# One encoder layer: seven block products for the gate tiles behind attention, token mixes made during attention, the second FFN matrix mixed beside its own products

## The chip, the cores and the metric

The kernel runs on one core of a Trainium2 chip. The metric is the device time of one execution in microseconds (us). Engines carry the profile's names: PE is TensorE (matmuls; PEld its weight loads), DVE VectorE, ACT ScalarE, POOL GpSimd, SP SyncE, on whose queue nearly all transfers are issued.

## The reference

One layer on 1024 tokens of 1024 channels: a modulated norm, one projection to queries, keys, values and gates, two attentions (a neighbourhood of a 2-D grid, and sliding windows of three dilations), a merge of both by sigmoid gates, an output projection, and a SwiGLU feed-forward network (FFN) of width 2816.

```
h = rms_norm(x, g_norm1) * (1 + sc1) + sh1
qa, ka, va, qb, kb, vb, gates = split(h @ w_in)
...
gate_a, gate_b = split(sigmoid(gates + b_gate), 2)
merged = gate_a * (o_a @ w_proj_a) + gate_b * (o_b @ w_proj_b)
x = x + gt1 * (merged @ w_o)
h2 = rms_norm(x, g_norm2) * (1 + sc2) + sh2
a, up = split(h2 @ w_ffn_in, 2)
x = x + gt2 * ((silu(a) * up) @ w_ffn_out)
```

## The kernel before

**Precision.** Everything is float32. For a matmul each operand is split into a high and a low half of a rounded float32 (`wsplit`: the high half is a copy on ACT, L108; the low half is a subtraction on POOL or DVE, L109), and each product is three passes, hi x hi, hi x lo, lo x hi (`PASS`). A matmul takes 128 x 128 weights and 512 moving columns.

**Buffers.** A weight comes by SP into a ring of 6 buffers `raw` (`wload`, L101), and its halves stand in rings of 10 each, which is five steps of two operands. PSUM has four names (ps_s, ps_t, ps_v, ps_d) of two banks. Pools lie on the left or on the right side of the core's memory.

**Order.** TensorE's queue is kept in the order of the program. On DVE, ACT, POOL and SP a scheduler orders the instructions at build time, among those that are ready by its own simulation; each queue then runs in that order, so an instruction that waits holds up all behind it. What is marked with `keep_in_program_order` (pinned, below) stays in the program's order on its engine.

**Stages.** (1) x is normalised and transposed into hT (8 row groups of 128 channels, 1024 tokens, a high and a low tile). (2) Steps n = 0 to 91, eight to a unit (units 2 to 4 are n = 16 to 39), interleave the projections (L293), attention (L442 scores, L468 transposes of P, L472 the copies PT, L483 the products with the values) and small work, such as the norms of q and k (L311 to L316) and the columns of the modulation (L282). The last steps also compute half gates (L602) for the first channel tiles, kept in DRAM. (3) Behind attention, `gates` computes the other gate tiles: for tile i and branch br, one product of 8 row groups for each half of the tokens: 24 matmuls each (L580, `mm_set`), a sigmoid from PSUM. Beside it run `w2_combos`, which load the four blocks of the second FFN matrix a group, make four mixes and store them to DRAM, for 11 groups; `w1_combos`, the same for two groups of the first matrix; and at its end `o_split`, which splits the attention's output into oT. (4) The merge (L580 on oT), (5) the output projection, (6) the first FFN matrix, (7) the second.

**Seven products.** Both FFN matrices are multiplied by Winograd's form of Strassen's method: of a product of 2 x 2 blocks, seven block products of mixed operands instead of eight, with sums of the results. In the second matrix (`prod2`) one of the seven has 11 steps k, each of two operands (mixed activations from `ga_d`, and a block or a mix of the matrix), with four tiles m of 3 matmuls. The seven run one after the other, and DVE sums them from PSUM into four quadrants c11 to c22. `finish` multiplies a quadrant by gt2 on DVE (L1266), adds x on POOL (L1267) and stores it. In the last product the three last steps run tile by tile, and each tile ends with a multiplication, a sum and a store (L1298, L1299).

Of the kernel before, what the change touches and what calls it, by code (L numbers as in the profile page):

```python
# [27 lines left out]
LATE = (3, 4, 5, 6, 7)  # L28
# [4 lines left out]
NLAND = 22  # L33
W2C = {0: (0,), 1: (1,), 2: (2, 3), 3: (4,), 4: (5,), 5: (6, 7), 6: (8,), 7: (9,), 8: (10,)}
# [9 lines left out]
def hybrid_layer(ctx: ExitStack, tc: tile.TileContext, x, colp, wada1, wada2, bada2, wqkv, wg, wpa, wpb,  # L44
# [539 lines left out]
    NPRE = 11  # L584

# [27 lines left out]
    gw, gsig = {}, {}  # L613
    units = []
# [144 lines left out]
    for n in range(6, 92):  # L759
# [67 lines left out]
    for br in range(2):  # L827
        gate_w(3, br)
    ap_.release()

    sgp = pool("sig", "right")
    sig = {}

    def sig_tile(i, br):
        z = sgp.tile(wide, F32, tag="sg", bufs=10, name="sg")
        for hf in range(2):
            sig.setdefault((i, br, hf), z[:, hf * 512:hf * 512 + 512])
# [4 lines left out]
    sig[2, 1, 1] = sgp.tile([128, 512], F32, name="s2")  # L842
    lnd = pool("land", "right")

    def gates(i, br):
        gate_w(i, br)
        for hf in range(2):
            hs = slice(hf * 512, hf * 512 + 512)
            if i * 4 + br * 2 + hf < NPRE:
                continue  # L850
            pb = bank("ds"[br])
            for j in range(2):
                mm_set(pb, gw[i, br][j], hT, 4 * j, 4, 8, 4 * j, hs)
            nc.scalar.activation(sig[i, br, hf], pb, AF.Sigmoid, bias=bg_c[:, 8 * br + i:8 * br + i + 1])

    def sig_load(i, br, hf):
        if i * 4 + br * 2 + hf < NPRE:
            hs = slice(hf * 512, hf * 512 + 512)
            nc.sync.dma_start(sig[i, br, hf], sig_d[i, br][:, hs])
            nc.scalar.activation(sig[i, br, hf], sig[i, br, hf], AF.Sigmoid)  # L860
# [7 lines left out]
    def merge(i):  # L868
        merge_w(i)
        wa, wb = mw[i]  # L870
        for hf in range(2):
            hs = slice(hf * 512, hf * 512 + 512)
            ppa, ppb = bank("tv"[hf]), bank("ds"[hf])
            mm_set(ppa, wa, oT, 0, 4, 4, 0, hs)
            mm_set(ppb, wb, oT, 4, 2, 2, 0, hs)
# [7 lines left out]
    def o_split():  # L883
        for pr in (4, 5, 0, 1, 2, 3):
            for hf in range(2):
# [3 lines left out]
                hi, lo = oT[0][:, pr, hs], oT[1][:, pr, hs]  # L889
                if pr < 4:  # L890
                    hi, lo = (z[:, pr].rearrange("p (r w) -> p w r", r=16)[:, 32 * hf:32 * hf + 32] for z in oT)
                    raw = raw.rearrange("p (w r) -> p w r", r=16)
                nc.scalar.activation(hi, raw, AF.Copy)
                (nc.gpsimd if hf else nc.vector).tensor_sub(lo, raw, fview(hi))

    def w2_combos(k):
        b = {}
        for r in range(2):
            for c in range(2):
                b[r, c] = lnd.tile([128, 512], F32, tag="l", bufs=NLAND, name="l")  # L900
# [504 lines left out]
```

## Time and profile before

| what | value |
|---|---|
| median of 3 runs | 1545.73 us (1543.94 to 1547.7) |
| profiled execution: time, span | 1547.32 us, 1545.5 us |
| granted clock | 0.999 |
| busy: PE, DVE, ACT, POOL | 1523.5, 1009.0, 652.5, 635.5 us |
| gates behind attention | 628.22 to 742.72 us, 504 matmuls |
| second FFN matrix | from 1331.2 us to the end |

The span is the profile's, from the first instruction to the last; the execution's time has about 2 us more. A row of a group names line, engine, operation, output and inputs, count, then busy time and the mean of one in ns. In a timeline a row with x3 is three instructions run together.

### The profile page before, as it was taken

The numbers are of one execution on the slowest core, as the hardware profiler recorded it, in microseconds if no ns is written. First come the engines' busy times: TensorE is split into PE (matmuls) and PEld (weight loads), VectorE is DVE, ScalarE is ACT, GpSimd is POOL, SyncE is SP. The second block draws the span as 40 slices with busy tenths as digits, with TensorE's granted clock in tenths as the row PEclk, the third lists the DMA queues.
The fourth block names the chain that finished last, engine by engine and source line by source line (L and its number), as shares of the span: only waits on it lengthen the run. The fifth ranks groups of instructions, "written<-read, shape, count | busy, mean of one in ns | idle before, by whom it ended". The sixth has DMA issues, their size and how long they took to land.

```text
span 1545.5 us, 24656 instructions
## 1 busy us (share of the span) xinstructions
PE 1523.5 (99%) x8216; PEld 1280.4 (83%) x8216; DVE 1009.0 (65%) x2230; ACT 652.5 (42%) x1702; POOL 635.5 (41%) x618
## 2 busy tenths in 40 slices
PE   9999999999999999999999999999999999999998
PEld 7988888898888877888888888888888888888887
DVE  6776676776889843333475488678867776434477
ACT  5564555555545453224342254223322233344433
POOL 0422331221000031565352220577777777545555
PEclk9999999999999999999999999999999999999999
DMA  9323231443344252896445234344543334576765
GB/s 364 125 85 98 62 117 44 129 132 112 89 132 144 90 174 71 276 382 234 133 136 200 82 109 141 122 153 156 171 135 104 107 105 133 197 217 197 246 216 199
DMA packets 153950, 236.42 MB, mean 153 GB/s; under 512 B 27856, under 2 KB 65616, under 8 KB 153824
## 3 DMA queue, kind: packets, MB, share of 16 engines
q1 hardware_dynamic: 153824, 234.85, 47.1%
q8 instruction: 65, 1.06, 0.3%
q14 instruction: 61, 0.50, 0.1%
HBM read 175.95 MB, written 58.83 MB: 152 GB/s over the span
## 4 chain that ended last, share of the span: by engine, by line
PE 88%; DVE 4%; DMA 3%; issue 2%; ACT 2%; POOL 0%; SPq 0%; DVEq 0%; POOLq 0%; ACTq 0%
PE ps_d L293 14%; PE ps_v L1091 7%; PE ps_d L1091 7%; PE ps_s L1091 7%; PE ps_t L1091 6%; PE ps_s L580 5%; PE ps_d L580 4%; PE ps_d L602 4%; PE ps_d L1247 4%; PE ps_s L1247 4%; PE ps_v L1247 3%; PE ps_t L1247 3%; PE ps_v L483 2%; PE ps_s L442 2%; PE ps_d L1027 2%; PE ps_s L1027 2%
## 5 line engine op out<-in xcount | busy, mean ns | idle before, releaser
L109 POOL TENSOR_TENSOR wlo<-raw,whi 128x512 fp32r<-128x512 f32 (+2 forms) x214 | 281.6, 1323 | 483.5 <-ACT whi L108 403.0
L108 ACT ACTIVATE whi<-raw 128x512 fp32r<-128x512 f32 (+1 forms) x382 | 222.0, 601 | 272.6 <-PE ps_s L1247 42.4
L293 PE MATMUL ps_d<-whi,hT 128*128 128x384 f32 x1152 | 317.8, 344 | 1.3 <-ACT v L328 1.3
L109 DVE TENSOR_TENSOR wlo<-raw,whi 128x512 fp32r<-128x512 f32 (+1 forms) x168 | 155.7, 938 | 100.2 <-ACT whi L108 88.3
L293 PEld LDWEIGHTS ps_d<-whi,hT 128*128 128x128 f32 x1152 | 211.1, 189 | 7.0 <-ACT vs L331 3.5
L293 PE MATMUL ps_d<-wlo,hT 128*128 128x384 f32 x576 | 194.0, 337 | 0.0
L293 PEld LDWEIGHTS ps_d<-wlo,hT 128*128 128x128 f32 x576 | 108.9, 189 | 0.2 <-POOL wlo L109 0.2
L1041 POOL TENSOR_TENSOR e<-e,c 128x512 f32<-128x512 f32 x44 | 67.8, 1541 | 47.9 <-DVE c L1171 25.0
L108 ACT ACTIVATE whi<-ws 128x512 fp32r<-128x512 f32 x60 | 37.8, 630 | 116.3 <-DVE ws L1108 55.0
L323 POOL TENSOR_TENSOR ra<-qn,rtab 128x64 f32<-128x64 f32 x48 | 16.4, 342 | 167.2 <-DVE qn L316 125.5
L457 ACT ACTIVATE P<-P,st 128x256 f32<-128x256 f32 (+2 forms) x100 | 46.2, 463 | 69.5 <-DVE st L456 69.4
L314 DVE TENSOR_REDUCE ss<-sq 128x4 f32<-128x256 f32 x80 | 33.3, 416 | 47.4 <-ACT sq L311 47.3
L1091 PE MATMUL ps_v<-h2T,whi 128*128 128x512 f32 x192 | 59.3, 390 | 0.0
L1091 PE MATMUL ps_s<-h2T,whi 128*128 128x512 f32 x192 | 59.2, 390 | 0.0
L483 PE MATMUL ps_v<-PT,v 128*64 128x128 f32 (+1 forms) x672 | 55.0, 284 | 2.1 <-DVE PT L472 2.1
L1091 PE MATMUL ps_d<-h2T,whi 128*128 128x512 f32 x184 | 56.9, 390 | 0.0
L1039 ACT ACTIVATE e<-e 128x512 f32<-128x512 f32 x44 | 27.4, 630 | 69.2 <-DVE e L1174 47.3
L457 ACT ACTIVATE P<-P,sx 128x384 f32<-128x384 f32 (+1 forms) x64 | 37.1, 580 | 46.3 <-DVE sx L456 46.3
L468 PE MATMUL ps_t<-ident,P 128*128 128x128 f32 (+1 forms) x336 | 51.7, 275 | 4.0 <-DVE P L460 1.7
L442 PE MATMUL ps_s<-qk 64*128 64x256 f32 (+3 forms) x492 | 53.8, 321 | 1.8 <-DVE st L456 1.2
L602 PE MATMUL ps_d<-hT,whi 128*128 128x512 f32 x176 | 55.4, 396 | 0.0
L442 PEld LDWEIGHTS ps_s<-qk 64*128 64x128 f32 (+1 forms) x492 | 35.0, 182 | 23.7 <-issue 11.5
(369 smaller groups left out, 3913.9 us busy)
## 6 DMA issues: line engine op xcount, KB each, us to landing
raw<-in_w_dram SPq DMA_DIRECT2D x139, 256.0 KB
ga_d<-e SPq DMA_DIRECT2D x77, 256.0 KB
raw<-ga_d SPq DMA_DIRECT2D x77, 256.0 KB
wa<-in_wada_dram SPq DMA_DIRECT2D x32, 512.0 KB
raw<-in_wqkv_dram SPq DMA_DIRECT2D x80, 192.0 KB
l<-in_w_dram SPq DMA_DIRECT2D x52, 256.0 KB
w_d<-l SPq DMA_DIRECT2D x52, 256.0 KB
raw<-w_d SPq DMA_DIRECT2D x52, 256.0 KB
```

The lines of the kernel that those rows point to most:

```text
L108: nc.scalar.activation(hi[:, :n], r, AF.Copy)
L109: (eng or nc.gpsimd).tensor_sub(lo[:, :n], r, fview(hi[:, :n]))
L293: nc.tensor.matmul(pd[:, :384], tok(a, k, t), U.w[k][b][:, :384], start=(k == 0 and i == 0), stop=(k == KT - 1 and i == 2))
L442: nc.tensor.matmul(I.pS[h][:nq, :nk], U.qk[a][hs, I.q0:I.q0 + nq], U.qk[2 + b][hs, I.kb0 * 128:I.kb0 * 128 + nk], start=(i == 0), stop=(i ...
L457: nc.scalar.activation(P[:nq, :nk], P[:nq, :nk], AF.Exp, scale=-1.0, bias=nm, accum_out=sm)
L483: nc.tensor.matmul(po[hs, :nq], U.v[:, I.kb0 + i, hs], I.PT[h][:, i, :nq], start=(i == 0), stop=(i == nkb - 1))
L580: nc.tensor.matmul(pb, wsl[a][:, j * 128:(j + 1) * 128], src[b][:, ksrc + j, hs], start=(done == 0 and j == 0 and i == 0), stop=(done + j ...
L602: nc.tensor.matmul(st["p"], gw[i, br][j][a][:, kk * 128:(kk + 1) * 128], hT[b][:, k, hs], start=(k == 0 and q == 0), stop=(k == 7 and q == 2))
L1027: nc.tensor.matmul(pbs[hf], h2T[a][:, k, t * 128:(t + 1) * 128], wow[hf, k][b], start=(n == 0 and (a, b) == PASS[0]), stop=(n == KT - 1 an ...
L1041: nc.gpsimd.tensor_mul(sg, sg, up)
L1091: nc.tensor.matmul(pb, w[p][:, k * 128:(k + 1) * 128], b[q][:, k], start=(k == 0 and i == 0), stop=(k == 3 and i == 2))
L1247: nc.tensor.matmul(pb[m], o[0][a][:, m * 128:(m + 1) * 128], o[1][b], start=(k == 0 and i == 0), stop=(k == HT - 1 and i == 2))
```

## The change

**Gates.** Tiles 3 to 7 are computed by seven products a tile. The 2 x 2 blocks of the weights are two branches by two halves of the row groups; those of hT are two halves of the row groups by two halves of the tokens. A product has 4 row groups and 12 matmuls (`gate_mm`). The weight mixes are made on DVE for each tile (`gate_mixes`). The four mixes of hT are made once, in `t_piece`, which is called for 24 steps from n = 18 on: eight groups of three pinned pieces (two sums; three subtractions and a copy to the high half; two subtractions for the low half and two stores of 512 KB to `t_d`). Behind attention three pairs of tiles (`ttp`, right side) and one quarter of hT itself are loaded from `t_d`. DVE sums the products from PSUM, ACT adds the bias and takes the sigmoid of 1024 columns. Tiles 6 and 7 run interleaved, and the buffers of `ttp`, once free, hold oT. All low halves of `o_split` are on DVE. NPRE goes from 11 to 12: half gate (2, 1) of the second half of the tokens is computed in step n = 91.

**First FFN matrix.** The two `w1_combos` go from the gates' stage to n = 85 and 88, all on DVE.

**Second FFN matrix.** `w2_combos`, their stores and the later loads from `w2_d` go. `w2_mix` loads four blocks of a group during the second and third product, mixes them with four subtractions on DVE, and keeps the mixes in memory. The three products on unmixed blocks come first, with both operands' low halves on DVE; the last quadrant is now c21.

The diff, cut to its core ("..." where lines are left out):

```diff
@@ constants @@
-NLAND = 22
-W2C = {0: (0,), 1: (1,), 2: (2, 3), 3: (4,), 4: (5,), 5: (6, 7), 6: (8,), 7: (9,), 8: (10,)}
+TP0 = 18
+LATE, NPRE = (3, 4, 5, 6, 7), 12
@@ new helpers before the units @@
+    def gate_raw(i, q):
+        return wload(wg[i, :, 4 * q:4 * q + 4, :], 512)
+
+    def gate_mm(pb, w, b, k):
+        for q, (x, y) in enumerate(PASS):
+            nc.tensor.matmul(pb, w[x][:, k * 128:(k + 1) * 128], b[y][:, k],
+                             start=(k == 0 and q == 0), stop=(k == 3 and q == 2))
+    def t_piece(m):
+
+        (kk, pc), part = divmod(m // 3, 2), m % 3
+        if part == 0:
+            tpc["t"] = [big("tp", [128, 4, 256], F32R) for _ in range(2)]
+        hi, lo = tpc["t"]
+        y = fview(lo)
+        pin = tc.keep_in_program_order
+        if part == 0:
+            for c in range(2):
+                cs = slice(512 * c + 256 * pc, 512 * c + 256 * pc + 256)
+                pin(nc.vector.tensor_add(y[:, 2 * c:2 * c + 2], *(fview(h[:, kk:8:4, cs]) for h in hT)))
+        elif part == 1:
+            pin(nc.vector.tensor_sub(y[:, 0:3:2], y[:, 2:4], y[:, 0:3:2]))
+            pin(nc.vector.tensor_sub(y[:, 3], y[:, 3], y[:, 0]))
+            pin(nc.vector.tensor_sub(y[:, 1], y[:, 1], y[:, 3]))
+            pin(nc.scalar.activation(hi, y, AF.Copy))
+        else:
+            for a in (0, 2):
+                pin(nc.vector.tensor_sub(lo[:, a:a + 2], y[:, a:a + 2], fview(hi[:, a:a + 2])))
+            for q, z in enumerate((hi, lo)):
+                nc.sync.dma_start(t_d[q, :, :, kk, 256 * pc:256 * pc + 256].rearrange("s p c -> p s c"), fview(z))
@@ the steps of the units @@
+        if TP0 <= n < TP0 + 24:
+            t_piece(n - TP0)
+        if n in (85, 88):
+            w1_combos((n - 85) // 3, EARLY[(n - 85) // 3])
@@ behind attention @@
+    def gate_first(i, eng):
+        for q, nm in enumerate(("w11", "w12")):
+            gwt[i, nm] = wsplit(gate_raw(i, q), eng)
+
+    def gate_mixes(i, order):
+        r = {q: gate_raw(i, q) for q in (0, 2, 3, 1)}
+        s1 = wp.tile([128, 512], F32, tag="raw", bufs=NRAW, name="ws")
+        nc.vector.tensor_sub(r[0], r[0], r[2])
+        nc.vector.tensor_add(s1, r[2], r[3])
+        nc.vector.tensor_sub(r[2], r[3], r[0])
+        nc.vector.tensor_sub(r[1], r[1], r[2])
+        z = {"x1": s1, "x2": r[2], "x3": r[0], "w22": r[3], "x4": r[1]}
+        for nm in order:
+            gwt[i, nm] = wsplit(z[nm], nc.vector)
+    GORD, GLATE = ("x2", "x3", "x1", "w22", "x4"), ("w22", "x3", "x2", "x1", "x4")
+    for i in (3, 4):
+        gate_first(i, None)
+    tbg = {"w11": hblk(0, 0), "w12": hblk(1, 0), "x4": hblk(1, 1), "x1": hblk(0, 1)}
+    for nm in ("w22", "x3", "x2"):
+        tbg[nm] = [ttp.tile([128, 4, 512], F32R, tag="t", bufs=6, name="tg") for _ in range(2)]
+    for n, nm in ((3, "x2"), (2, "x3"), (0, "x1"), (1, "w22")):
+        for q in range(2):
+            nc.sync.dma_start(fview(tbg[nm][q]), t_d[q, n])
+    def gate_prod(i, nm, late=False):
+        ng[0] += 1
+        p = bank("tvds"[ng[0] % 4])
+        for k in range(4):
+            gate_mm(p, gwt[i, nm], tbg[nm], k)
+        c11, c12, c21, c22 = sig[i, 0, 0], sig[i, 0, 1], sig[i, 1, 0], sig[i, 1, 1]
+        add = nc.vector.tensor_add
+        if nm == "w11":
+            nc.scalar.activation(c12, p, AF.Copy)
+        elif nm == "w12":
+            add(c11, c12, p)
+        elif nm == "x4":
+            add(c12, c12, p)
+        elif nm == "w22":
+            if late:
+                nc.scalar.activation(c21, p, AF.Copy)
+            else:
+                add(c21, c21, p)
+        elif nm == "x3":
+            if late:
+                add(c21, c21, p)
+                nc.scalar.activation(c22, p, AF.Copy)
+            else:
+                add(c21, c12, p)
+        elif nm == "x2":
+            add(c12, c12, p)
+            if late:
+                add(c21, c21, c12)
+                add(c22, c22, c12)
+        else:
+            add(c22, c22 if late else c21, p)
+            add(c12, c12, p)
+
...
-    def w2_combos(k):
-        b = {}
-        for r in range(2):
-            for c in range(2):
-                b[r, c] = lnd.tile([128, 512], F32, tag="l", bufs=NLAND, name="l")
-                nc.sync.dma_start(b[r, c], w2[(k + HT * r) * 128:(k + HT * r + 1) * 128, c * 512:c * 512 + 512])
-        t1, t3, t2, t4 = b[0, 0], b[0, 1], b[1, 1], b[1, 0]
-        nc.gpsimd.tensor_sub(t1, b[0, 1], b[0, 0])
-        nc.vector.tensor_sub(t3, b[1, 1], b[0, 1])
-        nc.gpsimd.tensor_sub(t2, b[1, 1], t1)
-        nc.vector.tensor_sub(t4, b[1, 0], t2)
-        for n, z in enumerate((t1, t2, t3, t4)):
-            nc.sync.dma_start(w2_d[n, k], z)
...
-    GS = [(2, 1)] + [(i, br) for i in LATE for br in range(2)]
-    for n, z in enumerate(GS):
-        for y in GS[n:n + 3]:
-            gate_w(*y)
-        gates(*z)
-        for k in W2C.get(n, ()):
-            w2_combos(k)
-        if n in (3, 6):
-            w1_combos(n // 6, EARLY[n // 6])
-        if n == max(W2C):
-            lnd.release()
-            op_ = pool("o", "right")
-            oT = [op_.tile([128, 6, S], F32R, name=f"oT{i}") for i in range(2)]
-            o_split()
+    gate_first(5, nc.vector)
+    for i in (3, 4):
+        firsts(i)
+    gate_mixes(3, GORD)
+    firsts(5)
+    for i in (3, 4):
+        gate_first(i + 3, nc.vector)
+        for nm in GORD:
+            gate_prod(i, nm)
+        gate_end(i)
+        gate_mixes(i + 1, GORD)
+        firsts(i + 3)
+    for nm in GORD:
+        gate_prod(5, nm)
+    gate_end(5)
+    gate_mixes(6, GLATE)
+    gate_mixes(7, GLATE)
+    for nm in GLATE:
+        for i in (6, 7):
+            gate_prod(i, nm, True)
+    oT = {}
+    o_split()
+    for i in (6, 7):
+        gate_end(i)
@@ second FFN matrix @@
+    def w2_mix(k):
+        b = [w2p.tile([128, 512], F32, name=f"m{n}_{k}") for n in range(4)]
+        for z, (r, c) in zip(b, ((0, 0), (0, 1), (1, 1), (1, 0))):
+            nc.sync.dma_start(z, w2blk(r, c, k))
+        t1, t3, t2, t4 = b
+        nc.vector.tensor_sub(t1, t3, t1)
+        nc.vector.tensor_sub(t3, t2, t3)
+        nc.vector.tensor_sub(t2, t2, t1)
+        nc.vector.tensor_sub(t4, t4, t2)
+        w2m[k] = t1, t2, t3, t4
-    PRODS = ((0, lambda k: w2blk(0, 0, k)), (4, lambda k: w2_d[1, k]), (1, lambda k: w2blk(1, 0, k)),
-             (5, lambda k: w2_d[2, k]), (3, lambda k: w2_d[0, k]), (2, lambda k: w2_d[3, k]),
-             (6, lambda k: w2blk(1, 1, k)))
+    PRODS = ((0, (0, 0)), (1, (1, 0)), (6, (1, 1)), (4, 1), (3, 0), (5, 2), (2, 3))
+        g, m = PRODS[n]
+        a = wload(ga_d[g, k], 512)
+        b = w2m[k][m] if n > 2 else wload(w2blk(*m, k), 512)
+        return wsplit(a, nc.vector), wsplit(b, nc.vector if n < 3 or k == HT - 1 or (n == 6 and k > 4) else None)
+            if n in (1, 2) and k % 2 == n - 1:
+                w2_mix((k + (n - 1) * HT) // 2)
...
+    p7 = prod2(5)
+    for m in range(4):
+        add(c21[m], c21[m], p7[m])
+        add(c22[m], c22[m], p7[m])
     finish(1, 1, c22)
-    p4 = prod2(5)
-    for m in range(4):
-        nc.vector.tensor_add(c21[m], c21[m], p4[m])
-    finish(1, 0, c21)
-    finish(0, 1, c12, True)
-    p3 = prod2(6)
+    finish(1, 0, c21, True)
+    p4 = prod2(6)
     for m in range(4):
         tm = fp.tile([128, 512], F32, tag="tm", bufs=4, name="tmf")
-        nc.vector.tensor_mul(tm, p3[m], gt2[:, 512:])
-        nc.vector.tensor_add(tm, tm, c12[m])
-        nc.sync.dma_start(out[m * 128:(m + 1) * 128, 512:], tm)
+        nc.vector.tensor_mul(tm, p4[m], gt2[:, :512])
+        nc.vector.tensor_add(tm, tm, c21[m])
+        nc.sync.dma_start(out[(m + 4) * 128:(m + 5) * 128, :512], tm)
```

Where the instructions move, on three queues; `L` numbers are those of the kernel named.

VectorE in attention, step n = 18. Before (`ss4` and `rz` belong to the norms of q and k, `acc2` to the modulation's columns, `PT` is the copy of the transposed P):

```order
L314 TENSOR_REDUCE ss4_1940<-sq_1937 128x4
L263 TENSOR_TENSOR row_1927<-ps_t_1925,brow_1928 1x512
L280 TENSOR_SCALAR acc2_1934<-wa2_1932,cact_95 128x512
L120 TENSOR_SCALAR rv_1942<-ss4_1940 128x4
L282 SCALAR_TENSOR_TENSOR acc2_1934<-wa2_1932,cact_95,acc2_1934 128x512
L122 TENSOR_TENSOR rz_1944<-ry_1943,rv_1942 128x4
```

And of the change (`tp` is a piece of mixed tokens):

```order
L313 TENSOR_REDUCE ss4_1940<-sq_1937 128x4
L262 TENSOR_TENSOR row_1927<-ps_t_1925,brow_1928 1x512
L279 TENSOR_SCALAR acc2_1934<-wa2_1932,cact_95 128x512
L119 TENSOR_SCALAR rv_1942<-ss4_1940 128x4
L281 SCALAR_TENSOR_TENSOR acc2_1934<-wa2_1932,cact_95,acc2_1934 128x512
L637 TENSOR_TENSOR tp_2037<-hT0_105,hT1_390 128x512
L121 TENSOR_TENSOR rz_1944<-ry_1943,rv_1942 128x4
L637 TENSOR_TENSOR tp_2037<-hT0_105,hT1_390 128x512
L122 SCALAR_TENSOR_TENSOR rz_1944<-rz_1944,ry_1943 128x4
```

The piece's two sums stand among the small operations of a norm.

VectorE in the second product of the second FFN matrix, of the change, the row that follows ScalarE's first copy of product 1 (`wlo_15418`) and on (`m0_2` is the first mix of group 2):

```order
L108 TENSOR_TENSOR wlo_15418<-raw_15411,whi_15417 128x512
L1331 TENSOR_TENSOR m1_2_15446<-m2_2_15447,m1_2_15446 128x512
L1332 TENSOR_TENSOR m2_2_15447<-m2_2_15447,m0_2_15445 128x512
L108 TENSOR_TENSOR wlo_15438<-raw_15433,whi_15437 128x512
L1333 TENSOR_TENSOR m3_2_15448<-m3_2_15448,m2_2_15447 128x512
L108 TENSOR_TENSOR wlo_15442<-raw_15435,whi_15441 128x512
...
L1333 TENSOR_TENSOR m3_10_15956<-m3_10_15956,m2_10_15955 128x512
L108 TENSOR_TENSOR wlo_15618<-raw_15613,whi_15617 128x512
L108 TENSOR_TENSOR wlo_15622<-raw_15615,whi_15621 128x512
```

The last two rows are the low halves of that product's eleventh step; the mixes of all eleven groups stand ahead of them. Before, no mix stood on this queue in this stage.

SyncE where the second matrix begins, of the change (`ga_d` from `e` is a store of the first matrix's last results):

```order
L1146 DMA ga_d_75<-e_14840 128x512
L1146 DMA ga_d_75<-e_14821 128x512
L100 DMA raw_15313<-ga_d_75 128x512
L1146 DMA ga_d_75<-e_14975 128x512
L100 DMA raw_15315<-in_w2_dram 128x512
L100 DMA raw_15349<-ga_d_75 128x512
L100 DMA raw_15351<-in_w2_dram 128x512
L1328 DMA m0_0_15325<-in_w2_dram 128x512
L1328 DMA m1_0_15326<-in_w2_dram 128x512
```

The first load of a mix stands behind the last of these stores and behind the raw buffers of the second product's second step.

More of the change, by code (lines that the diff above doesn't have):

```diff
@@ L825, in hybrid_layer @@
             proj_post(U, t)
-    for br in range(2):
-        gate_w(3, br)
+    def gate_first(i, eng):
[14 more added lines that the diff above has]
+        gate_first(i, None)
     ap_.release()
     sgp = pool("sig", "right")
+    ttp = pool("tt", "right")
     sig = {}
+    tbg = {"w11": hblk(0, 0), "w12": hblk(1, 0), "x4": hblk(1, 1), "x1": hblk(0, 1)}
[4 more added lines that the diff above has]
+            nc.sync.dma_start(fview(tbg[nm][q]), t_d[q, n])
     def sig_tile(i, br):
@@ L841, in hybrid_layer, with sig_load, gate_end @@
             sig_tile(i, br)
[L842 to L860, printed above, removed]
+    def sig_load(i, br):
+        z = sig_tile(i, br)
+        nc.sync.dma_start(z, sig_d[i, br])
+        nc.scalar.activation(z, z, AF.Sigmoid)
+    ng = [0]
+    def gate_prod(i, nm, late=False):
[30 more added lines that the diff above has]
+            add(c12, c12, p)
+    def gate_end(i):
+        for br in range(2):
+            z = sig[i, br]
+            nc.scalar.activation(z, z, AF.Sigmoid, bias=bg_c[:, 8 * br + i:8 * br + i + 1])
     mw = {}
@@ L873, in merge @@
             ppa, ppb = bank("tv"[hf]), bank("ds"[hf])
-            mm_set(ppa, wa, oT, 0, 4, 4, 0, hs)
-            mm_set(ppb, wb, oT, 4, 2, 2, 0, hs)
+            for pb, w, prs in ((ppa, wa, (0, 1, 2, 3)), (ppb, wb, (4, 5))):
+                for j, pr in enumerate(prs):
+                    for q, (a, b) in enumerate(PASS):
+                        nc.tensor.matmul(pb, w[a][:, j * 128:(j + 1) * 128], oT[pr][:, b, hs],
+                                         start=(j == 0 and q == 0), stop=(j == len(prs) - 1 and q == 2))
             m, sb = sig[i, 0, hf], sig[i, 1, hf]
@@ L884, in o_split @@
         for pr in (4, 5, 0, 1, 2, 3):
+            oT[pr] = ttp.tile([128, 2, S], F32R, tag="t", bufs=6, name="oT")
             for hf in range(2):
@@ L963, in hybrid_layer @@
         for z in MSIG.get(n, ()):
-            sig_tile(*z)
-            for hf in range(2):
-                sig_load(*z, hf)
+            sig_load(*z)
         if n + 2 < 8:
@@ L972, in hybrid_layer @@
             wo_keep(MKEEP[n])
-    op_.release()
+    ttp.release()
     wop = pool("wo", "right")
@@ L1209, in hybrid_layer @@
         late_weights(j)
-    for j in EARLY + tuple(i for k in range(len(EARLY) // 2, HT) for i in (k, k + HT)):
+    for n, j in enumerate(EARLY + tuple(i for k in range(len(EARLY) // 2, HT) for i in (k, k + HT))):
         if j not in EARLY[:2]:
@@ L1227, in w2blk @@
         return w2[(k + HT * r) * 128:(k + HT * r + 1) * 128, c * 512:c * 512 + 512]
[L1229 to L1231 removed]
+    w2p = pool("w2m", "right")
+    w2m = {}
+    def w2_mix(k):
[9 more added lines that the diff above has]
+    PRODS = ((0, (0, 0)), (1, (1, 0)), (6, (1, 1)), (4, 1), (3, 0), (5, 2), (2, 3))
     LASTK = 3
     def operands(n, k):
[L1235 to L1236 removed]
+        g, m = PRODS[n]
+        a = wload(ga_d[g, k], 512)
+        b = w2m[k][m] if n > 2 else wload(w2blk(*m, k), 512)
+        return wsplit(a, nc.vector), wsplit(b, nc.vector if n < 3 or k == HT - 1 or (n == 6 and k > 4) else None)
     def blocks(name):
```

70 lines of the change are left out of this document (40 added, 30 removed).

## The prediction

> **What bounds the kernel now.** I read the page first (span, busy row, shares of the chain of waits), then the chain in order of time around the gates, then windows of the stages that the change touches, and last the timelines of VectorE, ScalarE and SyncE at the second FFN matrix.
>
> ```profile
> span 1545.5 us, 24656 instructions
> PE 1523.5 (99%) x8216; PEld 1280.4 (83%) x8216; DVE 1009.0 (65%) x2230; ACT 652.5 (42%) x1702; POOL 635.5 (41%) x618
> PE 88%; DVE 4%; DMA 3%; issue 2%; ACT 2%; POOL 0%; SPq 0%; DVEq 0%; POOLq 0%; ACTq 0%
> ```
>
> TensorE is busy for 99% of the span. Everything else is either hidden by matmuls or one of the few stalls among them. So a change gains where matmuls go, and loses where an operand of a matmul comes later than its matmul.
>
> The chain in order of time (start, length, engine, tile, line, count), end of attention to the merge; the two rows at 97x and 98x are from the first FFN matrix:
>
> ```profile
> 618.04 5.46 PE ps_d L602 x24
> ...
> 628.22 5.71 PE ps_s L580 x24
> 633.92 10.88 PE ps_d L580 x48
> ...
> 731.84 10.88 PE ps_s L580 x48
> 742.72 2.81 PE ps_t L580 x12
> ...
> 974.27 2.81 PE ps_v L1091 x12
> ...
> 982.61 2.73 PE ps_t L1091 x12
> ```
>
> The gates behind attention are one unbroken run of matmuls from 628.22 to 742.72: 114.5 us for 24 + 10 x 48 = 504 of them. Two prices show. On hT a matmul costs 10.88/48 = 0.2267 us; on oT, a tile of the right side of the memory, 2.81/12 = 0.2342. The rows of the first FFN matrix have the same pair: 2.81 where the moving operand is a mixed tile, 2.73 where it is h2T.
>
> The windows (stretch, length, then busy us and count of PE, PEld, DVE, ACT, POOL, then granted clock, DMA share, GB/s):
>
> ```profile
> 20.00:24.00 4.00, 4.00 (x44) 3.11 (x48) 2.46 (x7) 3.41 (x8) 0.00 (x0) 1.00 1.04 398
> 133.00:290.00 157.00, 152.87 (x1079) 135.76 (x1076) 105.56 (x375) 84.23 (x318) 42.63 (x111) 1.00 0.33 100
> 450.00:500.00 50.00, 49.97 (x363) 43.63 (x362) 47.29 (x159) 26.24 (x88) 3.19 (x3) 1.00 0.47 140
> 628.00:685.00 57.00, 57.00 (x255) 47.04 (x252) 21.95 (x19) 14.41 (x22) 37.80 (x28) 1.00 0.99 358
> 690.00:700.00 10.00, 10.00 (x46) 8.29 (x45) 3.75 (x4) 1.38 (x2) 7.08 (x6) 1.00 1.05 393
> 1331.00:1361.00 30.00, 30.00 (x134) 24.86 (x133) 12.87 (x14) 14.86 (x25) 19.82 (x15) 1.00 0.82 273
> 1361.00:1391.00 30.00, 30.00 (x134) 24.86 (x133) 9.51 (x15) 13.34 (x24) 13.20 (x10) 1.00 0.70 202
> ```
>
> In the gates (628 to 685) TensorE never stops and VectorE is idle for more than half, but the DMA engines are full (0.99). In both products of the second FFN matrix (1331 to 1391) nothing is near its limit: one product takes 30 us, VectorE works 10 to 13 of them.
>
> **The change, part by part. Gates.** Seven products of 4 x 3 = 12 matmuls on four row groups, 84 a tile, take the place of two halves a branch, 96; five tiles make 420 for 480. The 24 matmuls of half gate (2,1) move into the tail of attention, where the row at 618.04 prices them at 5.46. Of the 420, products w11, w12, x4 and x1 read hT itself (240 x 0.2267 = 54.4); x2, x3 and w22 read tiles of the right side, like oT (180 x 0.2342 = 42.2). Sum: 5.5 + 54.4 + 42.2 = 102.0 against 114.5, **-12.5 us**. Had all 420 the higher price it would be 114.5 - 5.5 - 98.4 = -10.7, with the lower -13.8.
>
> What must hide under these matmuls: the weight mixes, lo halves and sums of a tile, about 18 VectorE operations of 0.6, 11 us of the 84 x 0.23 = 19.3 that a tile lasts; the 6 MB of mixed tokens, at the 393 GB/s of 690:700, 16 us, the first pair of them, x2's, after a third of that plus some 4 for the release of attention's memory, about +10, where x2 is wanted after six products of 2.72, at +16.3; the split of o, whose three pairs of buffers come free 22, 16 and 11 us before the gates' end. In exchange the 44 loads and 44 stores of the second matrix's mixes (22 MB) leave, which filled the DMA engines here. I cost the covers at 0; had x2's pair landed last of the three, at 4 + 16 = +20, the price would be 4.
>
> **Pieces in attention.** Eight groups of three pinned pieces in steps n = 18 to 41, one a step. A group has five VectorE operations of 512 elements a partition and two of 256, one ScalarE copy of 1024 and two stores. The prices:
>
> ```profile
> L316 DVE TENSOR_TENSOR qn<-qn,ry 128x256 f32<-128x256 f32 x80 | 34.4, 429 | 2.8
> 1479.39 0.68 DVE L1287 TENSOR_TENSOR c<-c,ps_d 128x512 f32<-128x512 f32 x1
> 1479.98 0.68 DVE L1288 TENSOR_TENSOR c<-c,ps_d 128x512 f32<-128x512 f32 x1
> ```
>
> The last two start 0.59 apart, so a row of 512 costs about 0.6 and one of 256 between 0.33 (half of 0.68) and 0.43. A group is 5 x 0.6 + 2 x 0.33 = 3.7, all eight 29.6 us. The window 133:290 holds these steps: VectorE goes from 105.6 to 135 of 157, from 67 to 86%. A VectorE queue is kept in order, so behind a piece wait the norms of q and k, the maxima of the scores and the copies PT, which the next step's matmuls need. The bounds are 0 and 29.6/2 = 14.8, half of it exposed. I take +1, since the window 450:500 shows the same kind of steps with VectorE 95% busy and TensorE still at 49.97 of 50. The clause moving the first matrix's mixes into n = 85 and 88 puts eight operations there; I cost it at 0 behind 618.04's matmuls, at 4 if bare.
>
> **Second matrix.** The 44 subtractions of 11 groups now stand in product 2, and the first three products split both operands on VectorE. By the new order all of them come before the last lo half of product 2: 44 + 21 VectorE rows in that product, 44 + 18 loads on SyncE. A product's step is 30/11 = 2.73, so that lo is due 21 x 2.73 = 57.3 us after the first product began at 1331.2. The rows of the start:
>
> ```profile
> 1331.20 0.39 PE L1247 MATMUL ps_d<-whi 128*128 128x512 f32 x1
> 1347.23 2.12 SPq L1053 DMA_DIRECT2D ga_d<-e  x2
> 1349.43 0.38 SPq L101 DMA_DIRECT2D raw<-w_d  x1
> 1359.44 1.12 ACT L1274 ACTIVATE c<-ps_d 128x512 f32<-128x512 f32 x2
> ```
>
> VectorE: ScalarE evacuates the first product at +28.2 (1359.44), and in the new order the hi half of product 2's fourth step stands behind the first of those copies. The lo of that half is row 2212 of VectorE, at about +29.2; 50 rows follow to the one that is due, 50 x 0.597 = 29.9: +59.1, 1.8 late. DMA: the first mix load stands on SyncE behind the first matrix's last stores, which end at 1347.23 + 2.12 = +18 here, and behind the raw buffers of product 2's second step; I take +15.5, between +13.6 (a ring's step earlier) and +20. Then 62 x 262 KB at 393 GB/s, 0.667 each, is 41.4, landing 3.1 (the span's end less the last operation at 1541.72 + 0.69) and the two halves of the split 1.2: +61.2, 3.9 late. Both limits lie close to the due time, one above the other, not summed. I take **+3**; ends 1.4 (start at +13.6 with 398 GB/s: 13.6 + 40.8 + 4.3 = +58.7) and 11.5, worked out with the rivals.
>
> The Trainium skill, DMA: Bandwidth & Descriptors, Where 436 GB/s comes from, says that for transfers between HBM and SBUF the HBM side binds, at about 358 GB/s a core. By that the 62 loads take 45.4 us, 4 more, and the whole would end near 1543. The rows 398 and 393 above, loads and loads with stores of this kernel alone on its core, disagree with it, so the sum keeps 393; a lower rate as a mechanism is the first rival, priced from a row of this case.
>
> The last product:
>
> ```profile
> 1487.68 4.08 DVE L1266 TENSOR_TENSOR c<-c,gt 128x512 f32<-128x512 f32 x3
> 1520.03 10.38 DVE L109 TENSOR_TENSOR wlo<-raw,whi 128x512 fp32r<-128x512 f32 x8
> 1531.19 2.73 DVE L109 TENSOR_TENSOR wlo<-raw,whi 128x512 fp32r<-128x512 f32 x4 [0.78 <-ACT whi L108]
> 1536.81 4.09 PE ps_s L1247 x18
> 1541.72 0.69 DVE L1299 TENSOR_TENSOR tmf<-tmf,c 128x512 f32<-128x512 f32 x1
> PEld ps_v L1247 <- DVE wlo L109: 0.2, 1, 0.2
> ```
>
> At 1520 eight lo halves run back to back, so VectorE is behind there, and TensorE's whole wait for it is 0.2. The change finishes two quadrants here (c22 and c21) in place of one: four more sums of 0.6 and four more multiplications, 0.6 alone and 4.08/3 = 1.36 beside GpSimd: 4.8 to 7.8 us more in the same queue. Against it, the lo halves that GpSimd contended for (1.3 instead of 0.7) gain about 3.3. Net 1.5 to 4.5, of which the wait shows what is beyond the slack; I take **+1.5**, ends 0 and 4.7. After it the same multiply, add and store end the span.
>
> Sum: -12.5 + 1 + 3 + 1.5 = **-7.0**, on the profiled execution's 1547.3 (1545.5 span and 1.8 around it): 1540.3. That execution lies 1.6 above the median of 1545.73, so the forecast beside the median is 1545.7 - 7.0 = **1539 us**.
>
> **Rivals.** *The second product starves on loads.* At the rate of 1331:1361, 273 GB/s at share 0.82, a full queue is 273/0.82 = 333: 62 x 0.787 = 48.8, with 15.5 + 4.3 gives +68.6, 11.5 late. For it: these loads share the engines with stores there. Against: 393 with stores in the gates. Net -12.5 + 1 + 11.5 + 1.5 = +1.5, or, starting at +20 with 393 and the last product at 4.7, -12.5 + 1 + 8.4 + 4.7 = +1.6: no change, 1546 to 1547. Chance 0.22.
>
> *The pieces stall attention.* In-order VectorE puts its extra 29.6 us before work that matmuls wait for. Half exposed is 14.8 in place of 1: -7.0 + 13.8 = +6.8, 1552. It turns the sign from a loss of 8 on, some 27% of the pieces. For it: in 133:290 TensorE already misses 4.1 of 157. Against: 450:500. Chance 0.14.
>
> *Everything is hidden.* The loads start before +12 and VectorE's rows don't stand behind the evacuation; the pieces and the last product's rows fit their slack: -12.5 alone, 1533. Chance 0.06. *The products don't get cheaper than the matmuls they drop*: with every matmul at the right side's price, -10.7, it is 1541, inside the forecast.
>
> **How the numbers follow.** Forecast (-10 to -3.1) 0.58, everything hidden 0.06, no change 0.22, attention stalls 0.14. About 0.2%, 3.1 us, is what a measurement of this kernel tells from no change: faster 0.64, same 0.22, slower 0.14. The likeliest case alone reaches from 1535.5 to 1542.5; the range reaches down to everything hidden and up past no change into the stall's lower half, 1533 to 1549.
>
> **What would show it.** Gates: from the first product to the merge 96 to 99 us, with no gap over 1 us; products x2, x3 and w22 at 2.81 per 12, the rest at 2.72. Attention: steps 18 to 41 take 157 to 159; over 165 and the pieces are the rival. Second matrix: a wait of TensorE for a lo half at the end of product 2 of 1 to 8 us, none over 1 in product 3. Last product: its last phase waits 0 to 5 for lo halves. I am wrong if the gates save under 10, or if a wait over 3 us stands where this text has none.

## The result, and the profile after

The changed kernel takes 1560.26 us (median of 4 runs, 1557.91 to 1562.35) against 1546.72 for the kernel before, run beside it: a ratio of 1.0087, 95% interval 1.0064 to 1.0111. It is some 13.5 us slower, where 7 us faster was forecast; the range ended at 1549.

The page of the changed kernel (span, busy time of the engines):

```profile
span 1558.3 us, 24622 instructions
PE 1517.8 (97%) x8156; PEld 1272.4 (82%) x8156; DVE 1116.0 (72%) x2444; ACT 671.9 (43%) x1719; POOL 533.8 (34%) x540
```

TensorE has 5.7 us less to do and the span is 12.8 us longer, so it now waits. Where, is seen from the first and last start of each stage's matmuls. The view of one line gives count, shortest, median and longest duration in ns, then first and last start. Of the kernel before, the projections:

```profile
L293 PE MATMUL ps_d<-whi,hT x1152: 334/334/669, 67.9 to 542.0; 128*128 128x384 f32 x192
```

Of the changed kernel, the projections and the first row of the gates:

```profile
L292 PE MATMUL ps_d<-whi,hT x1152: 333/334/668, 67.9 to 554.9; 128*128 128x384 f32 x192
L618 PE MATMUL ps_v<-hT,whi x48: 389/389/395, 646.5 to 737.8; 128*128 128x512 f32 x48
```

Read so for every stage (profiled executions, us):

| stage | before | after | change | forecast |
|---|---|---|---|---|
| to the end of the projections | 542.0 | 554.9 | +12.9 | +1 |
| from there to the first gate product | 86.1 | 91.6 | +5.5 | +5.5 |
| gates | 114.5 | 97.2 | -17.3 | -18.0 |
| merge to the end of the first FFN matrix | 588.6 | 588.6 | 0 | 0 |
| second matrix: product 2 | 29.9 | 41.0 | +11.1 | +3 |
| last product | 29.7 | 30.4 | +0.7 | +1.5 |

The gates saved what was forecast, 11.8 with the half gate that moved. Two other places took 24 us back. The waits of TensorE in the changed kernel (what waited for what, us in total, times, longest) name them:

```profile
PE ps_v L350 <- POOL qn L325: 10.6, 6, 6.1
PE ps_v L1354 <- ACT whi L107: 5.9, 3, 4.0
...
PE ps_t L618 <- DMA tg<-t_d: 0.3, 1, 0.3
```

The last row is the whole price of loading the mixed tokens: that cover held.

**Attention.** The store of v that each step issues gives the steps' times. The changed kernel is level with the one before up to step 22 (within 0.6 us), 2.7 us behind at step 23, 9.7 at step 24, and 15 from step 42 on. TensorE and VectorE there (start, length, engine, line; in brackets the idle time before, and its releaser):

```profile
179.69 0.69 PE L350 MATMUL ps_v<-ident,qn 128*128 128x128 f32 x2 [6.06 <-POOL qn L325]
```

```profile
164.30 0.17 DVE L119 TENSOR_SCALAR rv<-ss 128x4 f32<-128x4 f32 x1
165.91 1.49 DVE L281 SCALAR_TENSOR_TENSOR acc<-wa,cact,acc 128x512 f32<-128x512 f32 x1 [1.44 <-DMA wa<-in_wada_dram]
167.33 1.28 DVE L637 TENSOR_TENSOR tp<-hT,hT 128x512 f32<-128x512 f32 x2
...
169.00 0.97 DVE L121 TENSOR_TENSOR rz<-ry,rv 128x4 f32<-128x4 f32 x1
...
171.91 0.68 DVE L639 TENSOR_TENSOR tp<-tp 128x512 f32<-128x512 f32 x1
...
173.31 0.17 DVE L122 SCALAR_TENSOR_TENSOR rz<-rz,ry 128x4 f32<-128x4 f32 x1
...
173.86 2.08 DVE L645 TENSOR_TENSOR tp<-tp 128x512 fp32r<-128x512 f32 x2
175.86 0.41 DVE L640 TENSOR_TENSOR tp<-tp 128x256 f32<-128x256 f32 x1
...
176.53 0.14 DVE L123 SCALAR_TENSOR_TENSOR ry<-rz,ry 128x4 f32<-128x4 f32 x1
...
177.89 0.41 DVE L315 TENSOR_TENSOR qn<-qn,ry 128x256 f32<-128x256 f32 x1
```

One norm of q and k is five small rows that depend on each other: rv, rz, rz, ry, qn. Pieces of the mixed tokens (tp) stand between them, and a multiplication of the modulation (acc) that waits for its load. From rv to qn it takes 13.6 us; in the kernel before, the same norm took 4.5:

```profile
163.69 0.17 DVE L120 TENSOR_SCALAR rv<-ss 128x4 f32<-128x4 f32 x1
...
168.19 0.41 DVE L316 TENSOR_TENSOR qn<-qn,ry 128x256 f32<-128x256 f32 x1
```

Of the 9.1 us more, the rows of the pieces take 4.5, and two multiplications of the modulation, with the wait, 3.5. The wait of 6.06 behind this norm is where the lateness goes from 2.7 to 9.7. Over the 24 norms of steps 18 to 41, the times from rv to qn add up to 54 us before and 83 in the changed kernel.

**Second matrix.** The chain of the changed kernel at the end of product 2, and its windows there:

```profile
1388.18 6.04 DMA raw<-in_w_dram
...
1394.33 0.64 ACT whi L107
...
1395.02 3.23 PE ps_v L1354 x6
1398.24 2.40 PE ps_t L1354 x6
1400.64 1.39 PE ps_v L1354 x6
```

```profile
1362.00:1403.00 41.00, 34.05 (x134) 26.20 (x133) 39.71 (x63) 15.68 (x26) 0.00 (x0) 0.92 1.00 366
```

The tenth step's second operand is issued at 1388.18, behind 40 of the 44 loads of mixes and 15 loads of operands since the first mix, and is in memory 6.04 later. In product 2 the transfers are full (share 1.00), and VectorE is nearly so (39.7 of 41).

### The profile page after: what moved, and what is told of

Its sections match the earlier page's. It is cut to its first block, busy times and chain, and to the rows that moved or that the text cites. A ratio compares the mean times of both kernels' runs of the same rounds, so it can differ in the third digit from the quotient of the medians.

```text
span 1558.3 us, 24622 instructions
## 1 busy us (share of the span) xinstructions
PE 1517.8 (97%) x8156; PEld 1272.4 (82%) x8156; DVE 1116.0 (72%) x2444; ACT 671.9 (43%) x1719; POOL 533.8 (34%) x540
## 5 line engine op out<-in xcount | busy, mean ns | idle before, releaser
L108 POOL TENSOR_TENSOR wlo<-raw,whi 128x512 fp32r<-128x512 f32 (+2 forms) x133 | 172.3, 1307 | 485.4 <-ACT whi L107 434.5
L107 ACT ACTIVATE whi<-raw 128x512 fp32r<-128x512 f32 (+1 forms) x348 | 205.1, 600 | 293.9 <-PE ps_t L1354 41.0
L108 DVE TENSOR_TENSOR wlo<-raw,whi 128x512 fp32r<-128x512 f32 (+1 forms) x215 | 178.7, 840 | 84.6 <-ACT whi L107 79.4
L107 ACT ACTIVATE whi<-ws 128x512 fp32r<-128x512 f32 x65 | 41.0, 631 | 126.1 <-DVE ws L1201 58.9
L108 POOL TENSOR_TENSOR wlo<-m,whi 128x512 fp32r<-128x512 f32 x35 | 49.5, 1416 | 53.5 <-ACT whi L107 53.4
L313 DVE TENSOR_REDUCE ss<-sq 128x4 f32<-128x256 f32 x80 | 33.1, 414 | 42.6 <-ACT sq L310 42.4
L599 PE MATMUL ps_d<-hT,whi 128*128 128x512 f32 x192 | 60.5, 396 | 0.0
L108 DVE TENSOR_TENSOR wlo<-ws,whi 128x512 fp32r<-128x512 f32 x45 | 49.7, 1104 | 8.2 <-ACT whi L107 8.2
```

What stands on the lines that cost most here:

```text
L107: nc.scalar.activation(hi[:, :n], r, AF.Copy)
L108: (eng or nc.gpsimd).tensor_sub(lo[:, :n], r, fview(hi[:, :n]))
L313: nc.vector.tensor_reduce(ss, sq.rearrange("p (h d) -> p h d", h=4), axis=mybir.AxisListType.X, op=ALU.add)
L599: nc.tensor.matmul(st["p"], gw[i, br][j][a][:, kk * 128:(kk + 1) * 128], hT[b][:, k, hs], start=(k == 0 and q == 0), stop=(k == 7 and q == 2))
```

## The experiments

Each profile is one execution; "projections end" is read as above, against 542.0 before.

**Pieces later** (e1).

```diff
-        if TP0 <= n < TP0 + 24:
-            t_piece(n - TP0)
+        if 79 <= n < 91:
+            for z in range(2):
+                t_piece(2 * (n - 79) + z)
```

> The changed kernel with one edit: the 24 pieces of mixed tokens are called two a step in n = 79 to 90, where VectorE was busy for 14 to 21 of 40 us, instead of one a step in n = 18 to 41. Theory A (in the dense steps the pieces fill VectorE's ordered queue, so that the norms of q and k come late, TensorE stops for up to 6 us and then runs at half its clock): the 12.8 us that attention lost come back, 1560.3 - 12.8 = 1547.5, and no wait over 1 us for qn stands in steps 18 to 41. Rival (the pieces cost the same wherever they stand, by their buffers in the ring or their 4 MB of stores, or the gates then wait for the tiles): attention and gates together still lose over 6, 1554 or more.

1557.46 us, ratio 1.0075 (1.0058 to 1.0092). The projections ended at 544.8, 2.8 late (0.7 of it from ahead of the units), so the loss does come from the pieces. But the rest of attention took 98.3 in place of the changed kernel's 91.6 and the gates 101.0 in place of 97.2, so 10.5 went again, as much as was gained (the profiled execution took 1561.59, above the median). Its window there, and two waits of TensorE:

```profile
545.00:643.00 98.00, 93.39 (x547) 72.14 (x546) 73.73 (x182) 43.50 (x97) 20.21 (x14) 0.98 0.73 234
```

```profile
PE ps_t L467 <- DVE P L459: 4.6, 4, 2.2
PE ps_t L618 <- DMA tg<-t_d: 1.9, 1, 1.9
```

VectorE was busy for only 74 of 98 us, and still TensorE waited for a row of it. The theory missed the total, and the rival was right about it: room on VectorE isn't enough.

**Mixes spread** (e2).

```diff
-            if n in (1, 2) and k % 2 == n - 1:
-                w2_mix((k + (n - 1) * HT) // 2)
+            if (n, k) in WMIX:        # (product, step): group; 4, 4 and 3 in products 2, 3 and 4
+                w2_mix(WMIX[n, k])    # its loads and subtractions pinned
```

> The changed kernel with one edit: the eleven groups of mixes of the second matrix are pinned in the program's order and spread, four in product 2, four in product 3, three in product 4 (each ahead of its use), so that a product has 16 to 12 mix loads beside its 22 of operands, at most 38 x 0.68 = 26 us of 30. Theory B (44 mix loads ahead of product 2's own operands): the 11.1 us of product 2 come back and nothing takes their place, 1560.3 - 11 = 1549. Rival (the loss is in splitting both operands on VectorE in products 1 to 3, or it moves to products 3 and 4): the second matrix still loses over 5, 1554 or more.

1553.15 us, ratio 1.005 (1.0034 to 1.0066). Product 2 took 29.9 again, so its 11.1 us came back, and 1.2 went over to product 4, which took 31.1. The total moved by 7 and not 11. The profiled execution took 1558.25, above the median, and in it the projections ended at 562.4, later than in the changed kernel's 554.9, though VectorE's order there is the same. Whether a later attention is also why the median gained less than 11 isn't shown. Its product 2:

```profile
1370.00:1400.00 30.00, 30.00 (x134) 24.86 (x133) 25.18 (x41) 14.60 (x26) 0.00 (x0) 1.00 0.99 345
```

The transfers are still full there, but the product's own operands no longer stand behind all the mixes.

**Loads or subtractions alone.** e4 leaves out the 44 subtractions, so its output isn't the layer's; e5 keeps them but loads only the first group's blocks, so its output isn't either.

```diff
-        nc.vector.tensor_sub(t1, t3, t1)
-        nc.vector.tensor_sub(t3, t2, t3)
-        nc.vector.tensor_sub(t2, t2, t1)
-        nc.vector.tensor_sub(t4, t4, t2)
```

```diff
-            nc.sync.dma_start(z, w2blk(r, c, k))
+            if k == 0:
+                nc.sync.dma_start(z, w2blk(r, c, k))
...
+        s1, s3, s2, s4 = b if k == 0 else w2raw   # the first group's tiles
```

> The changed kernel without the 44 subtractions of the mixes: their loads stay, and the last four products use unmixed blocks, so the output is not the reference's. Theory B (the transfers are what comes late in product 2): product 2 still ends 8 to 11 us late, 1557 to 1560. Rival (VectorE's queue, 98% busy there, is what comes late): product 2 ends less than 3 late, near 1551.

> The changed kernel with the 44 subtractions, but only the first group's four blocks loaded: the subtractions of the other ten groups read the first group's tiles, so the output is not the reference's. Theory B (transfers): product 2 ends less than 3 us late, near 1550. Rival (VectorE): it still ends 8 to 11 late, 1557 to 1560.

Product 2 took 42.4 us with the loads alone and 36.0 with the subtractions alone (one execution each). Their windows, e4 and then e5:

```profile
1365.00:1407.00 42.00, 34.55 (x132) 26.30 (x131) 14.37 (x22) 15.83 (x26) 0.00 (x0) 0.92 1.00 362
```

```profile
1360.00:1395.00 35.00, 29.82 (x129) 23.63 (x128) 35.00 (x59) 13.01 (x22) 0.00 (x0) 1.00 0.47 147
```

With VectorE two thirds idle the loss is whole, 12.5: the transfers set product 2. With half the transfers gone VectorE is busy for all 35 us, and 6.1 stay: it is a second bound right behind. This second number is rough, since e5's subtractions stand in another order than the changed kernel's, and start every 0.60 us where most of those start 0.72 apart. The theory is right on the first and wrong on the second, where it expected under 3. Neither relief alone was enough; the spread, which relieves both, was.

**Pieces not pinned** (e6).

```diff
-        pin = tc.keep_in_program_order
+        pin = (lambda z: z)
```

> The changed kernel with one edit: the pieces are not pinned, so the order of VectorE puts them up to some 130 rows earlier, where its own simulation found room. Theory A (the sheer work of the pieces in an ordered queue, wherever dense steps are): the projections still end 8 us or more later than before's 542.0. Rival (the pinning, which keeps a piece behind the instruction traced ahead of it, is what makes the norms late): they end less than 4 later.

Projections end 557.1, 15.1 late (1562.53 us, one execution). Pinning is not the cause; in VectorE's timeline rows of pieces stand inside ten norms here too, as in the changed kernel.

**Pieces away from the units' ends** (e7, with the mixes spread, the last groups a little earlier than in e2).

```diff
-        if TP0 <= n < TP0 + 24:
-            t_piece(n - TP0)
+        if n in TPN:                  # n = 18 to 53, second to sixth step of a unit
+            t_piece(TPN.index(n))
```

> Two edits of the changed kernel: the mixes of the second matrix spread over products 2 to 4 (as before, with the last three a little earlier), and the pieces still one a step, but only in the second to sixth step of a unit (n = 18 to 53), not in its last two and first, where the next unit's weights are split on VectorE. Theory A2 (the big wait falls where a piece meets those splits: +7 to +9 at the end of unit 2): attention loses under 5, the second matrix under 2, and the time is 1545.5 - 12 + 5 + 2 = 1540 or less. Rival (any 30 us of VectorE work in these units costs 13 to 20, however spread): the projections end 10 or more late and the time stays at 1549 or more.

1549.5 us, ratio 1.0019 (1.0008 to 1.003). The second matrix, from its first matmul to its last, took 210.2 against 209.3 before, as expected. The projections ended at 556.7. The wait at unit 2's end was gone, and others had come, 6.5 at step 30 and 5 at step 42. So the meeting with the weight splits was not the cause, and theory A2 falls. But here too rows of pieces stand between rv and qn: up to six in one norm, where the changed kernel has up to seven.

**Pieces without VectorE** (e9). The seven VectorE rows of a piece are left out, and ScalarE copies hT into both tiles instead, so the output is not the layer's.

```diff
-                pin(nc.vector.tensor_add(y[:, 2 * c:2 * c + 2], *(fview(h[:, kk:8:4, cs]) for h in hT)))
...
+                for z in (hi, lo):
+                    pin(nc.scalar.activation(z[:, 2 * c:2 * c + 2], fview(hT[0][:, kk:8:4, cs]), AF.Copy))
```

> The changed kernel with the pieces' seven VectorE operations left out (ScalarE copies hT into both tiles, so the output is not the reference's); the ring buffers, the stores and the loads stay. Theory A (VectorE): the projections end less than 3 us later than before's 542.0. Rival (the ring's buffers or the 4 MB of stores): they still end 8 or more later.

Projections end 549.1, 7.1 late (1554.5 us, one execution): between the two. So some of the loss goes with the VectorE rows, about half of 12.9. What stays may be the extra ScalarE copies, which stood ahead of the squares of the norm (2.2 us at 161.97), or the ring, that is the seven large buffers (`big`) of which the pieces take two and which also hold what the modulation loads; this run can't tell.

**Pieces behind the norm** (e10, e11). The same pieces in the same steps, called after `proj_post`, which holds the step's norm; so each is pinned behind that norm's last row. Mixes spread as in e7.

```diff
-        if TP0 <= n < TP0 + 24:
-            t_piece(n - TP0)
...
         if u < 10:
             proj_post(U, t)
+        if n in TPN:                  # e10 and e23: n = 18 to 41; e11: the steps of e7
+            t_piece(TPN.index(n))
```

> Mixes of the second matrix spread as in e7; the pieces again one a step in n = 18 to 41, but called at the end of a step, so that a piece is pinned behind the norm of that step's q and k instead of ahead of it. In VectorE's order no row of a piece then stands between the first and the last row of a norm; in the changed kernel up to five do. Theory A3 (a piece between the dependent small rows of a norm makes qn late; the work itself fits): the projections end less than 4 us later than before's 542.0, and the time is 1545.5 - 12 + 3 + 1 = 1537 to 1540. Rival (some 30 us more on VectorE in these units is too much in any order): the projections end 9 or more later, 1546 or more.

> As e10, but the pieces stand in the second to sixth step of a unit, n = 18 to 53, as in e7. Theory A3: the projections end less than 4 us later than before's, as in e10, where e7, with the same steps and the pieces ahead of the norms, ended 14.7 later. Rival (total work): 9 or more later, as in e7.

e10: 1542.01 us, ratio 0.9971 (0.996 to 0.9982), 0.3% faster than the kernel before, though short of the 1537 to 1540 expected; its product 3 took 31.9. e11: 1546.92, ratio 1.0001 (0.9991 to 1.0011). The projections, e7, e10 and e11:

```profile
L292 PE MATMUL ps_d<-whi,hT x1152: 333/334/669, 67.7 to 556.7; 128*128 128x384 f32 x192
```

```profile
L292 PE MATMUL ps_d<-whi,hT x1152: 333/334/589, 67.5 to 545.9; 128*128 128x384 f32 x192
```

```profile
L292 PE MATMUL ps_d<-whi,hT x1152: 333/334/668, 67.6 to 549.7; 128*128 128x384 f32 x192
```

With the same steps, 14.7 late became 7.7 (e7 to e11); at the change's own steps 12.9, or 20.4 with the mixes spread, became 3.9 (the changed kernel and e2 to e10). VectorE's order has no piece inside a norm any more, and the norm of the fence above is back at 4.5 us in e10, 164.12 to 168.62:

```profile
164.12 0.17 DVE L119 TENSOR_SCALAR rv<-ss 128x4 f32<-128x4 f32 x1
...
168.62 0.41 DVE L315 TENSOR_TENSOR qn<-qn,ry 128x256 f32<-128x256 f32 x1
168.96 0.68 DVE L639 TENSOR_TENSOR tp<-tp 128x512 f32<-128x512 f32 x1
```

Over the norms of steps 18 to 41, rv to qn adds up to 59 us in e10, where the changed kernel had 83. The work is unchanged, so the order is what cost most. The move also changed how many multiplications of the modulation stand inside the norms of steps 16 to 47 (18 rows before, 19 in the changed kernel, 12 in e10), so the pieces' share alone isn't separated. e11 missed its expectation of under 4. Two of its waits for qn are over 1 us: one of 1.8 stands behind a norm in which a multiplication waits 1.69 for its load; what makes the longer one, 2.1, isn't settled.

**Behind the norm alone** (e23), without the spread of the mixes:

> The changed kernel with one edit: the pieces are called at the end of a step, behind the norm, as in e10; the mixes of the second matrix stay as the change has them. Theory (two losses with nothing in common): attention as in e10, product 2 as in the changed kernel, 1542.0 + 11 = 1553. Rival (they share something): below 1549 or above 1557.

1552.67 us, ratio 1.0039 (1.0026 to 1.0052), as expected from two independent losses: projections end 548.0, product 2 took 40.7. Product 2 lost nearly as much as behind the late attention.

**The ring alone** (r1), on the kernel before:

```diff
+        if 18 <= n < 42:
+            if n % 3 == 0:
+                rh["t"] = [big("rh") for _ in range(2)]   # a pinned VectorE copy of 8 columns into each
+            elif n % 3 == 2:
+                for q, z in enumerate(rh["t"]):           # the copy again, then a store of 4 KB
+                    nc.sync.dma_start(rh_d[q], z[:, :8])
```

> The kernel before with one addition: in n = 18 to 41 two of the seven ring buffers are taken for three steps at a time, as the pieces take them, each with two VectorE copies of 8 columns and a store of 4 KB; no mixes of tokens. Theory R (what stays of attention's loss once the pieces stand behind the norms, 3.9 to 7.7 us in e10 and e11, comes from the ring: the modulation's loads and multiplications come later and fall into other steps): the projections end 2 to 6 us later than before's 542.0. Rival (the ring costs nothing, the rest is VectorE's work): less than 1 later.

1545.68 us, ratio 0.9995 (0.9985 to 1.0004); projections end 542.1. The ring costs nothing by itself, though it moved multiplications of the modulation in VectorE's order. Theory R falls, and what makes the 3.9 to 7.7 us that stay in e10 and e11 is open; r1 says only that holding the buffers doesn't make them.

**A more even spread** (e18: e10 with two edits; the second takes a piece's second buffer a step later):

```diff
-            (1, 0): 0, (1, 3): 1, (1, 6): 2, (1, 9): 3, (2, 0): 4, (2, 2): 5, (2, 4): 6, (2, 6): 7, (2, 8): 8, (3, 2): 9, (3, 5): 10
+            (1, 0): 0, (1, 3): 1, (1, 6): 2, (1, 9): 3, (2, 0): 4, (2, 3): 5, (2, 6): 6, (2, 9): 7, (3, 1): 8, (3, 3): 9, (3, 5): 10
...
-            tpc["t"] = [big("tp", [128, 4, 256], F32R) for _ in range(2)]
+            tpc["lo"] = big("tp", [128, 4, 256], F32R)
+        elif part == 1:
+            tpc["hi"] = big("tp", [128, 4, 256], F32R)
```

> e10 with the mixes spread more evenly over products 2 to 4 (every third step; the last three at steps 1, 3 and 5 of product 4) and a piece's second buffer taken one step later. Product 3 took 2.0 and product 4 0.6 more than 29.9 in e10: if the mixes' crowding in product 3 is the cause, both end within 0.5 and the time is 1540; if not, it stays at 1542 or moves to product 4.

1542.73 us, ratio 0.9973 (0.9961 to 0.9984), no different from e10. Product 3 took 29.9, product 4 31.0: the last 1 us had moved on, as in e2.

**The order of attention, taken together.** The end of the projections varies from profile to profile, so a single one can mislead. With the pieces ahead of the norms, the same order of attention was profiled four times (e5, the changed kernel, e4, e2): 10.4, 12.9, 15.4 and 20.4 late. With the pieces behind them and the same steps, three times (e18, e10, e23): 3.7, 3.9 and 6.0. The two groups don't overlap.

## Why the prediction was wrong

- **What bounds the kernel** held: TensorE's queue, and the lateness of its operands.
- **Gates** held: -17.3 for the stage and +5.5 for the half gate, -11.8 in place of -12.5. The covers costed at 0 cost 0.3.
- **The step that failed first is the price of the pieces, "I take +1".** It compared busy shares: 86% after, against a window 95% busy with no wait. But a share says nothing on the order. The small rows of a norm depend on each other, and a long row between each two of them adds its whole length to the norm. In 450 to 500 of the kernel before, norms took up to 5.4 us from rv to qn and TensorE did not wait for them; behind the one of 13.6 it waited 6.06. The excerpt ahead of the prediction showed it, pieces among the rows of rz; I counted the work and not where it stood. Half exposed, 14.8, was the bound, and the rival that the pieces stall attention gave 1552 for it, with a chance of 0.14. Its 14.8 lies close to the 12.9 by luck: half was no more than a bound, and the same order lost 10.4 to 20.4. What it named, work ahead of what matmuls wait for, was the place; e10 and e11 showed that the order sets most of the price.
- **Product 2, "I take +3", was mis-sized.** The mechanism and the bound by transfers were right, and the rate too: the 56 loads up to the late operand were issued in 38.55 us, 0.70 each, against 0.667. The start was +17.3, taken as +15.5. A load under this traffic landed 6.04 after its issue, where I used 3.1, that of the last store in an idle queue. So the tenth step's operand came at +62.7 with its split, 8.1 after its due time of 20 x 2.73 = +54.6; by my numbers 2.6. I had also checked the eleventh step only. TensorE's waits of 0.70, 0.23, 1.17, 0.81 and 4.04 are 7.0 of the 11.1, and the slow clock behind them another 2.9 (3.23 and 2.40 for six matmuls that take 1.36). Of the 1.2 left, 1.0 is in how a wait is counted: from the end of a matmul's row, 0.39 to 0.49 long, where at full clock the next row starts 0.23 after the start of the last. The rival that starves on loads had 11.5, through a lower rate, which did not show: the windows from 1362 to 1392 have 385 to 390 GB/s.
- **VectorE's limit there** was mis-sized as well: 1.8 late was forecast, 6.1 stayed with the loads gone (e5). Its row price of 0.597 fits e5's 0.60; which of its other terms was wrong isn't shown.
- **The last product** cost 0.7 in place of 1.5, **product 3** nothing.
- **The clock had no term in the sum.** Behind the wait of 6.06 TensorE ran at half its clock; columns as in the windows of the prediction:

```profile
175.00:180.00 5.00, 0.31 (x2) 0.31 (x3) 4.28 (x17) 1.49 (x6) 1.54 (x6) 0.50 0.52 170
180.00:185.00 5.00, 5.00 (x19) 5.00 (x18) 0.88 (x3) 0.81 (x3) 0.65 (x3) 0.50 0.00 0
```

  In the second row TensorE is busy for all 5 us and does 19 matmuls, where 36 to 39 fit at full clock in the neighbouring stretches. So about 2.5 us follow on a wait of 6. The Trainium skill, TensorE: Matmul & The Clock Gate, What's actually happening, says that an idle window of some 3.4 us halves the clock, and that it returns after about as long of activity. The lengths agree: the traces have the clock at 0.50 for 10.2 us here, 6.8 in product 2 and 3.4 in e10. That it takes a wait of 3.4 does not show: here the clock fell 1.3 us into the wait, and in e10 a wait of 1.58 us was followed by 3.4 at 0.50 (181.8 to 185.2). By that page of the Trainium skill each long wait costs at least half of such a window more, an estimate of 1.7 us, where the rows show 2.5 and 2.9.
- **The chances** treated the two losses as rivals, one or the other. They don't depend on each other (e23), so both could happen, and did: with 12.9 and 11.1 in place of 1 and 3, the sum of -7.0 becomes +13.0, where the spans differ by 12.8.

## What to carry to other kernels

When work is added to an engine that runs its queue in order, read in the new order what stands between the rows of a dependent chain that the critical engine waits for, add those rows' lengths to the chain, and compare the sum with the time at which the critical engine needs the result; a busy share can't price it. Place such work behind the chain's last row; here that took away most of the loss, not all. When loads are added ahead of operands, cost each operand with the landing time of a full queue, check every step and not the last alone, and allow for the slow clock behind a wait, which came here after a wait of 1.6 us too.

## What the runs showed of the hardware

- Loads of 256 KB landed 5.4 to 6.1 us after their issue in product 2, at 385 to 390 GB/s; the kernel's last store, with nothing behind it, took 3.1.
- VectorE's subtractions of one group of mixes, which share tiles, started 0.72 us apart in product 2 (1388.65, 1389.37, 1390.09 for three in a row), with the DMA engines full. But rows in the same stretch that share no tile, such as the two weight splits from 1371.93 on and the two from 1386.84 on, started 0.60 apart, as did rows that read PSUM. So full DMA engines don't account for the 0.12; what does isn't shown.
- A row of four elements can wait for GpSimd: in the changed kernel the first rz row of a norm (`rz<-ry,rv`) took 0.14 to 0.18 us in all 58 cases with GpSimd idle, and over 0.5, up to 0.97, in 9 of the 12 that met one of its weight splits (the row at 169.00 above); in the kernel before, in 12 of 14.
- The same order of instructions in attention lost between 10.4 and 20.4 us to the end of the projections in four profiles (e5, the changed kernel, e4, e2). What differs between them isn't shown.
